# One weight block in four gets its low part from an accumulating DMA instead of a VectorE subtraction

## The chip, the core and the metric

The kernel runs on one core of one Trainium2 chip. The metric is the device time of one execution in microseconds (us). TensorE (PE in the profile) multiplies, VectorE (DVE), ScalarE (ACT) and GpSimd (POOL) work on vectors, SyncE (SP) issues the loads. Each engine takes its own queue of instructions in order and waits on semaphores for what the others make. Every DMA, whoever issues it, runs on the core's 16 DMA engines.

## The reference

Two layers, each of a feed-forward part, a mixer (a state space and an attention beside each other) and a second feed-forward part, over 256 tokens of width 1024, all in float32:

```python
for i in range(DEPTH):                                  # DEPTH = 2
    h = h + 0.5 * swiglu_ffn(rmsnorm(h, norm_ffn1[i]), w_ffn1_in[i], w_ffn1_out[i])
    u = rmsnorm(h, norm_mix[i]) @ w_mix_in[i]           # 1024 -> 6232
    ...
    h = h + jnp.concatenate([y_ssd, y_att], axis=-1) @ w_mix_out[i]
    h = h + 0.5 * swiglu_ffn(rmsnorm(h, norm_ffn2[i]), w_ffn2_in[i], w_ffn2_out[i])
return rmsnorm(h, final_norm)
```

The feed-forward width is 2816, so nearly all the work is the product of 256 tokens with some 208 MB of weights, each of which is read once.

## The kernel before

Each float32 weight is split into two float32r parts whose sum it is, and each main product is three matrix products: x_hi by w_hi, x_hi by w_lo, x_lo by w_hi (lines 181 to 183; 887 to 889 where the weight is the stationary operand).

The weights come as 203 blocks, numbered from 0 in the order of their use, nearly all of 128 partitions by 2048 columns (1 MB). `Stream` handles them. `load` (line 113) issues a block's load from SP into one of three `raw` buffers. `ahead` splits a block: ScalarE casts `raw` to `whi` (line 126), then VectorE makes `wlo` as `raw` minus `whi` (line 127). `whi` and `wlo` have three buffers each. `done` is called when the last product that reads a block has been written down, and it splits the block three further on, into the buffers that come free. So the cast of block b waits until TensorE has finished with block b-3, and the load of block b+3 waits until both readers of `raw` of block b are through.

The order in which TensorE uses the blocks sets how long it takes from a buffer's release to the need for its next content:

- A pair. In the input product of a feed-forward part and in most of the mixer's projection, two blocks (first half and second half of the 1024 rows) belong to the same 512 columns. TensorE reads first half, second half for tokens 0 to 127, then first half, second half for tokens 128 to 255. The first half is released after three quarters of the pair, the second after four. With three buffers, the release after three quarters goes to the second half of the next pair, and that is needed a quarter into that pair: two quarters later. The release after four quarters goes to the first half of the pair after the next, four quarters ahead of its use.
- An output block (256 rows by 1024 columns) is read once through, and is released when TensorE is through with it. The next content of its buffers is needed two blocks later; the last two of a product are read alternately, so that the second of them is needed sooner.

One part of the mixer's projection uses single blocks of 256 columns. The state space's dt chain runs on GpSimd (lines 597 to 610) and ends in a product at line 613. Beside the order of the buffers, a planner orders each engine's instructions by priority and expected times, apart from those that are pinned.

The functions the change touches, and what calls them:

Of the kernel before, what the change touches and what calls it, by code (L numbers as in the profile page):

```python
# [8 lines left out]
F32 = mybir.dt.float32  # L9
FR = mybir.dt.float32r  # L10
I32 = mybir.dt.int32
AF = mybir.ActivationFunctionType
ALU = mybir.AluOpType
AX = mybir.AxisListType

P = 128
D = 1024
# [20 lines left out]
def _pieces12(value, n):  # L38
    """value as n float32 parts of 12 significant bits each (the last one as it comes)."""
    import numpy as np  # L40

    parts, rest = [], float(value)
    for i in range(n):
        p = np.float32(rest)
        if i < n - 1:
            p = (p.view(np.uint32) & np.uint32(0xFFFFF000)).view(np.float32)
        parts.append(float(p))
        rest -= float(p)
    return parts
# [3 lines left out]
def hybrid_kernel(  # L53
# [6 lines left out]
    nc = tc.nc  # L60
# [12 lines left out]

# [1 line left out]
    def bank(pool):  # L75
# [4 lines left out]
    def pin(ins):  # L80
        """Where it matters, an engine takes its instructions in the order given here."""
        return tc.keep_in_program_order(ins) if strict[0] else ins

    def main_bank(wide):
        """The next bank of a main product: one of four, or of two."""
        turns[0] += 1
        return bank(ac if wide and turns[0] % 4 >= 2 else mm)
# [9 lines left out]

    class Stream:
        """The weights, a block at a time in the order of their use: loaded ahead, and split into
        two float32r parts whose sum they are."""  # L100

# [15 lines left out]
        def ahead(self, most=99):  # L117
            while most and self.split < min(self.freed + self.BLOCKS, len(self.plan)):
                self.load()
                n, raw = self.plan[self.split][0], self.raws.pop(0)  # L120
                hi = whl.tile([P, 2048], FR, name="whi", tag="whi")
                lo = whl.tile([P, 2048], FR, name="wlo", tag="wlo")
                parts = 2 if 3 <= self.split < 6 else 1
                for i in range(parts):
                    o = slice(i * n // parts, (i + 1) * n // parts)
                    pin(nc.scalar.copy(hi[:, o], raw[:, o]))  # L126
                    pin(nc.vector.tensor_sub(lo[:, o], raw[:, o], hi[:, o].bitcast(F32)))  # L127
                self.ready.append((hi, lo))
                self.split += 1
                most -= 1  # L130
# [4 lines left out]
        def done(self):  # L135
            """No product will read the oldest block any more."""
            self.freed += 1
            self.ahead()

    class Flow:  # L140
        """Work beside the main products: what was put off at one unit of those comes after the
        next one, and then some steps of the side work."""

# [32 lines left out]
    stream, flow = Stream(), Flow()  # L176

    def three(ps, xhl, t, whi, wlo, first, last):
        """ps += (xh + xl) @ (wh + wl), all but xl @ wl, which float32 does not hold."""
        xh, xl = (v[:, t * P:(t + 1) * P] for v in xhl)  # L180
        nc.tensor.matmul(ps, xh, whi, start=first, stop=False)  # L181
        nc.tensor.matmul(ps, xh, wlo, start=False, stop=False)  # L182
        nc.tensor.matmul(ps, xl, whi, start=False, stop=last)  # L183

# [1 line left out]
    HALVES = ((0, 4), (4, 8))  # L186
# [60 lines left out]
    def project(norm, n, wide=True):  # L247
        """x @ columns, by token: (t, result) as each is there."""
        hl = []
        for t in range(NT):  # L250
            ps = main_bank(wide)[:, :n]
            for i, (k0, k1) in enumerate(HALVES):
                if t == 0:
                    hl.append(stream.take())
                for k in range(k0, k1):
                    hi, lo = (v[:, (k - k0) * n:(k - k0 + 1) * n] for v in hl[i])
                    three(ps, norm.xT[k], t, hi, lo, k == 0, k == KD - 1)
                if t == NT - 1:
                    stream.done()
                if i == 0:  # L260
                    flow.step()
            yield t, ps

    def project_first(norm, n):
        """The same, as the first blocks come: both halves of the tokens side by side."""
        pss = [main_bank(True)[:, :n] for _ in range(NT)]
        for k0, k1 in FIRST:
            hl = stream.take()
            for k in range(k0, k1):
                hi, lo = (v[:, (k - k0) * n:(k - k0 + 1) * n] for v in hl)  # L270
                for t in range(NT):
                    three(pss[t], norm.xT[k], t, hi, lo, k == 0, k == KD - 1)
            stream.done()
        yield from enumerate(pss)

# [1 line left out]
    ones = const.tile([P, P], F32, name="ones")  # L277
    nc.gpsimd.memset(ones, 1.0)
    # the tensor engine is at work before the first operands are there, for its clock's sake
    idle = bank(sd)  # L280
    for _ in range(WARM):
        nc.tensor.matmul(idle[:, 0:P], ones, ones, start=True, stop=True)
    h_res = const.tile([P, NT, D], F32, name="h_res")
# [42 lines left out]

    # cos and sin of the rotary angles, by token: 16 of attention's and 8 of the index's;
    # by use: [cos | cos] and [-sin | sin]
    NF = 24
# [5 lines left out]
    def setup():  # L335
        """What the first products do not need."""
        def later(*a, **k):
# [61 lines left out]
    def rope(eng, v, t, which, nh):  # L399
        """v [P, nh, head dim], in place."""  # L400
        cc, ss, n = ropes[which]
        m1 = row1k()
        m2 = row1k()
        m1 = m1[:, :nh * 2 * n].rearrange("p (h c) -> p h c", h=nh)
        m2 = m2[:, :nh * 2 * n].rearrange("p (h c) -> p h c", h=nh)
        eng.tensor_tensor(m1, v[:, :, 0:2 * n], bc(cc[:, t], [P, nh, 2 * n], 1), ALU.mult)
        eng.tensor_tensor(m2[:, :, 0:n], v[:, :, n:2 * n], bc(ss[:, t, 0:n], [P, nh, n], 1), ALU.mult)
        eng.tensor_tensor(m2[:, :, n:2 * n], v[:, :, 0:n], bc(ss[:, t, n:2 * n], [P, nh, n], 1), ALU.mult)
        eng.tensor_tensor(v[:, :, 0:2 * n], m1, m2, ALU.add)

    def split_scaled(ps, parts, t):
        """Each 128 columns of a bank, times a gain by partition, as two float32r parts."""
        parts = [([v[:, t * P:(t + 1) * P] for v in hl], g, ps[:, i * P:(i + 1) * P])
# [6 lines left out]

# [1 line left out]
    def inv_rms(parts, n, name):  # L422
        """(sum of parts / n + eps) ** -0.5"""
        m = small.tile([P, 1], F32, name=f"ms_{name}", bufs=4)
# [16 lines left out]
    class Norm:  # L441
        """The residual stream, times the gain, as the next product's stationary operand; its
        rms comes into that product's result."""

# [25 lines left out]

# [1 line left out]
    def out_product(yT, n, scale, after, need=None):  # L472
        """h_res += scale * y @ w; yT by 128 rows of w; after(t, c) once a part is done."""
        acc = {}
# [38 lines left out]

# [1 line left out]
    def ffn(first, norm, after):  # L515
# [33 lines left out]

# [1 line left out]
    def mixer(l, norm, after):  # L551
        with ExitStack() as mctx:
# [28 lines left out]

# [1 line left out]
            def steps():  # L583
                """dt = softplus(.) as max(v, 0) + 2 atanh(e / (2 + e)), e = exp(-|v|); the sums of
                dt * a, by token and as rows."""
                if l == 0:
# [41 lines left out]

# [1 line left out]
            def index():  # L630
# [51 lines left out]

# [1 line left out]
            def conv(c, ps):  # L684
# [25 lines left out]

# [1 line left out]
            def ssd():  # L712
# [56 lines left out]
            def finish_y(g, half, pss):  # L769
                """D x, the gate, the norm and the transpose, each some time after the other."""  # L770
                sq = [None] * NT
# [31 lines left out]

# [1 line left out]
            def attention():  # L805
# [70 lines left out]

# [1 line left out]
            flow.until(lambda: not flow.side)  # L878
# [50 lines left out]

# [1 line left out]
    norm = Norm(0, 0)  # L931
# [74 lines left out]
```

## Time and profile before

| | before |
|---|---|
| time, median of 3 runs (lowest to highest) | 1229.9 us (1229.71 to 1231.31) |
| span of the profiled execution | 1227.5 us |
| TensorE matmuls busy | 1207.6 us (98%) |
| VectorE busy | 733.1 us (60%), 452.0 us of it in line 127 |
| ScalarE busy | 623.4 us (51%), 377.5 us of it in line 126 |
| GpSimd busy | 104.7 us (9%) |
| mean load on the DMA engines | 51.9% for SP's queue, 208.52 MB |

Busy times are sums over the whole span. A table like this tells which engine has no room left; it does not tell how long each block's parts are ready before TensorE wants them. That is read block by block in the timeline, below.

### The profile page before, as it was taken

How to read it: one execution, taken by the hardware profiler on the slowest of the kernel's cores; microseconds unless marked ns; L12 is line 12 of the kernel's file. 1: busy time of each engine (PE TensorE's matmuls, PEld its weight loads, DVE VectorE, ACT ScalarE, POOL GpSimd, SP SyncE). 2: the span in 40 equal slices, each digit the busy share in tenths (PEclk: the TensorE clock that was granted, in tenths of full speed). 3: DMA queues.
4: the chain of work that ended last, by engine and by line, in shares of the span. 5: the costliest groups of instructions: out<-in, count | busy, mean ns of one | idle time of the engine just before them, and what ended most of it. 6: DMA issues, size and time to landing. Idle time of an engine off the chain costs nothing.

```text
span 1227.5 us, 15384 instructions
## 1 busy us (share of the span) xinstructions
PE 1207.6 (98%) x6031; PEld 1010.6 (82%) x6031; DVE 733.1 (60%) x970; ACT 623.4 (51%) x856; POOL 104.7 (9%) x209
## 2 busy tenths in 40 slices
PE   8999999999899999999999999999989999999997
PEld 6788889988788888888888888898878888888886
DVE  5655545788478565554465554477766866555543
ACT  5544435556566454444354444365647755444432
POOL 0200000204230000000000000020152200000000
PEclk9999999999999999999999999999999999999999
DMA  8565555564333555655646645565444244556450
GB/s 260 192 206 181 188 175 168 193 202 142 105 136 106 169 184 165 200 198 179 202 152 195 197 168 202 158 212 173 156 154 137 86 172 157 176 182 206 175 202 35
DMA packets 147821, 210.02 MB, mean 171 GB/s; under 512 B 7909, under 2 KB 115109, under 8 KB 147749
## 3 DMA queue, kind: packets, MB, share of 16 engines
q1 hardware_dynamic: 147604, 208.52, 51.9%
q8 instruction: 47, 0.77, 0.3%
q10 hardware_dynamic: 144, 0.52, 0.1%
q14 instruction: 26, 0.20, 0.0%
HBM read 207.98 MB, written 1.05 MB: 170 GB/s over the span
## 4 chain that ended last, share of the span: by engine, by line
PE 90%; DVE 4%; POOL 2%; ACT 1%; issue 1%; DMA 1%; SPq 0%; POOLq 0%; ACTq 0%; DVEq 0%
PE mm L181 14%; PE mm L183 14%; PE mm L182 14%; PE ac L181 12%; PE ac L183 12%; PE ac L182 12%; PE tp L522 2%; DVE wlo L127 1%; PE ac L760 1%; PE sd L821 1%; PE ac L887 1%; PE tp L464 1%; PE mm L889 1%; PE mm L888 1%; PE mm L887 1%
## 5 line engine op out<-in xcount | busy, mean ns | idle before, releaser
L127 DVE TENSOR_TENSOR wlo<-raw,whi 128x2048 fp32r<-128x2048 f32 (+3 forms) x206 | 452.0, 2199 | 326.0 <-ACT whi L126 325.1
L126 ACT CAST whi<-raw 128x2048 fp32r<-128x2048 f32 (+3 forms) x206 | 377.5, 1837 | 303.8 <-PE ac L183 190.5
L181 PE MATMUL mm<-whi,tT 128*128 128x512 f32 (+1 forms) x672 | 269.2, 401 | 0.0
L183 PE MATMUL mm<-whi,tT 128*128 128x512 f32 (+1 forms) x672 | 262.4, 391 | 0.2 <-DVE tT L418 0.2
L182 PE MATMUL mm<-wlo,tT 128*128 128x512 f32 (+1 forms) x672 | 261.2, 389 | 0.0
L181 PE MATMUL ac<-whi,tT 128*128 128x512 f32 (+1 forms) x480 | 189.8, 396 | 1.0 <-ACT tT L416 0.5
L182 PE MATMUL ac<-wlo,tT 128*128 128x512 f32 (+1 forms) x480 | 185.2, 386 | 0.7 <-DVE wlo L127 0.7
L183 PE MATMUL ac<-whi,tT 128*128 128x512 f32 (+1 forms) x480 | 185.3, 386 | 0.0
L183 PEld LDWEIGHTS mm<-whi,tT 128*128 128x128 f32 x672 | 126.8, 189 | 26.3 <-DVE tT L418 0.5
L181 PEld LDWEIGHTS mm<-whi,tT 128*128 128x128 f32 x672 | 127.2, 189 | 25.6 <-issue 1.3
L182 PEld LDWEIGHTS mm<-wlo,tT 128*128 128x128 f32 x672 | 127.4, 190 | 23.0 <-DVE wlo L127 0.2
L182 PEld LDWEIGHTS ac<-wlo,tT 128*128 128x128 f32 x480 | 90.4, 188 | 17.7 <-DVE wlo L127 1.8
L183 PEld LDWEIGHTS ac<-whi,tT 128*128 128x128 f32 x480 | 90.2, 188 | 17.9
L181 PEld LDWEIGHTS ac<-whi,tT 128*128 128x128 f32 x480 | 90.2, 188 | 17.7 <-ACT whi L126 0.9
L432 POOL TENSOR_TENSOR r_x<-ms_x,mhalf 128x1 f32<-128x1 f32 x14 | 9.7, 694 | 873.0 <-DVE ms_x L430 865.4
L181 PE MATMUL ac<-whi,hT_hi 128*128 128x512 f32 x176 | 69.3, 394 | 0.0
L181 PE MATMUL mm<-whi,hT_hi 128*128 128x512 f32 x176 | 69.0, 392 | 0.0
L183 PE MATMUL ac<-whi,hT_lo 128*128 128x512 f32 x176 | 68.6, 390 | 0.0
L183 PE MATMUL mm<-whi,hT_lo 128*128 128x512 f32 x176 | 68.6, 390 | 0.0
L182 PE MATMUL ac<-wlo,hT_hi 128*128 128x512 f32 x176 | 68.5, 389 | 0.0
L182 PE MATMUL mm<-wlo,hT_hi 128*128 128x512 f32 x176 | 68.5, 389 | 0.0
L544 ACT ACTIVATE s1k<-ac,r_x 128x256 f32<-128x256 f32 x44 | 20.6, 471 | 67.6 <-PE ac L183 64.7
(220 smaller groups left out, 1447.3 us busy)
## 6 DMA issues: line engine op xcount, KB each, us to landing
raw<-in_w_ffn_in_dram SPq DMA_DIRECT2D x172, 512.0 KB, 5.0
raw<-in_w_ffn_out_dram SPq DMA_DIRECT2D x44, 1024.0 KB, 4.9
raw<-in_w_mix_in_dram SPq DMA_DIRECT2D x44, 1024.0 KB, 5.3
raw<-in_w_mix_out_dram SPq DMA_DIRECT2D x16, 1024.0 KB, 4.9
raw<-in_w_mix_in_dram SPq DMA_DIRECT2D x4, 600.0 KB, 3.9
raw<-in_w_mix_in_dram SPq DMA_DIRECT2D x4, 568.0 KB, 3.9
raw<-in_w_ffn_in_dram SPq DMA_DIRECT2D x8, 256.0 KB, 3.7
h_res<-in_x_dram SPq DMA_DIRECT2D x4, 256.0 KB, 3.9
```

The lines of the kernel that those rows point to most:

```text
L126: pin(nc.scalar.copy(hi[:, o], raw[:, o]))
L127: pin(nc.vector.tensor_sub(lo[:, o], raw[:, o], hi[:, o].bitcast(F32)))
L181: nc.tensor.matmul(ps, xh, whi, start=first, stop=False)
L182: nc.tensor.matmul(ps, xh, wlo, start=False, stop=False)
L183: nc.tensor.matmul(ps, xl, whi, start=False, stop=last)
L464: nc.tensor.transpose(ps[:, i * P:(i + 1) * P], src[:, i * P:(i + 1) * P], ident)
L522: nc.tensor.transpose(ps[:, f * L + t * P:f * L + (t + 1) * P], hs[:, t, f * P:(f + 1) * P], ident)
L544: nc.scalar.activation(sg, ps[:, 0:256], AF.Silu, scale=norm.r[t])
L760: nc.tensor.matmul(o, m0[:, h % 4, t * P:(t + 1) * P], half[:, 0, h * 64:(h + 1) * 64], start=True, stop=(t == 0))
L821: nc.tensor.matmul(ps[:, j * nk:(j + 1) * nk], qT[:, hg + h0 + j, t * P:(t + 1) * P], kT[:, hg + h0 + j, 0:nk], start=True, stop=True)
L887: nc.tensor.matmul(ps, hi[:, o:o + P], xh, start=(k == 0), stop=False)
L888: nc.tensor.matmul(ps, hi[:, o:o + P], xl, start=False, stop=False)
```

## The change

For blocks with a number above 16 that leaves 1 when divided by 4, and that have 2048 columns, the split is made in three steps: ScalarE casts `raw` to `whi` as before, ScalarE writes the negative of `whi` into `wlo`, and GpSimd issues a DMA that adds `raw` to `wlo` in place. The subtraction on VectorE is left out for these blocks. The changes of comments in the diff do nothing.

```diff
                 parts = 2 if 3 <= self.split < 6 else 1
+                if self.split > 16 and self.split % 4 == 1 and n == 2048:
+
+                    nc.scalar.copy(hi, raw)
+                    nc.scalar.activation(lo, hi.bitcast(F32), AF.Copy, scale=-1.0)
+                    nc.gpsimd.dma_start(lo, raw, accum_op=ALU.add)
+                    parts = 0
                 for i in range(parts):
                     o = slice(i * n // parts, (i + 1) * n // parts)
                     pin(nc.scalar.copy(hi[:, o], raw[:, o]))
                     pin(nc.vector.tensor_sub(lo[:, o], raw[:, o], hi[:, o].bitcast(F32)))
```

That picks 45 of the 203 blocks (37 and 137 are narrower than 2048): second halves of pairs in the second feed-forward parts (73, 77, 81, 85, 89 and 173 to 189), first halves in the first feed-forward parts (17, 21 and 105 to 121), in the projection the first halves 41, 45, 49 and the second halves 53, 57, 61 (141 to 161 in the second layer), and the output blocks 25, 29, 33, 65, 69, 93, 97, 101 (each again 100 later).

## Rows read from the trace of the kernel before

**Rows 1.** The page: busy us (share of the span) xinstructions, by engine.
```profile
PE 1207.6 (98%) x6031; PEld 1010.6 (82%) x6031; DVE 733.1 (60%) x970; ACT 623.4 (51%) x856; POOL 104.7 (9%) x209
```

**Rows 2.** Waits, all engines: engine line waited for: us in total, times, longest us.
```profile
DVE wlo L127 <- ACT whi L126: 325.1, 161, 5.7
...
PE sd L613 <- POOL adt L610: 7.0, 2, 3.5
...
PE ac L182 <- DVE wlo L127: 0.7, 1, 0.7
```

**Rows 3.** Waits of SP's own queue of DMAs.
```profile
SPq L113 <- DVE wlo L127: 774.6, 114, 15.2
```

**Rows 4.** Timeline, block 73: start, us, engine, line, operation [idle before <-releaser].
```profile
439.09 1.91 ACT L126 CAST whi<-raw 128x2048 fp32r<-128x2048 f32 x1 [0.37 <-PE mm L183]
...
441.03 2.29 DVE L127 TENSOR_TENSOR wlo<-raw,whi 128x2048 fp32r<-128x2048 f32 x1 [1.15 <-ACT whi L126]
...
444.87 0.39 PE L182 MATMUL mm<-wlo,tT 128*128 128x512 f32 x1
```

**Rows 5.** Timeline, block 189, the last of the ten like block 73.
```profile
1136.31 2.29 DVE L127 TENSOR_TENSOR wlo<-raw,whi 128x2048 fp32r<-128x2048 f32 x1 [3.24 <-ACT whi L126]
...
1140.11 0.39 PE L182 MATMUL mm<-wlo,tT 128*128 128x512 f32 x1
```

**Rows 6.** Timeline, block 69, last output block of the mixer.
```profile
414.57 2.29 DVE L127 TENSOR_TENSOR wlo<-raw,whi 128x2048 fp32r<-128x2048 f32 x1 [3.19 <-ACT whi L126]
...
419.41 0.39 PE L182 MATMUL mm<-wlo,tT 128*128 128x512 f32 x1
```

**Rows 7.** Timeline, block 57, a second half in the projection.
```profile
317.75 2.29 DVE L127 TENSOR_TENSOR wlo<-raw,whi 128x2048 fp32r<-128x2048 f32 x1 [5.74 <-ACT whi L126]
...
323.28 0.40 PE L182 MATMUL mm<-wlo,tT 128*128 128x512 f32 x1
```

**Rows 8.** Timeline, block 41, a first half in the projection.
```profile
214.73 2.29 DVE L127 TENSOR_TENSOR wlo<-raw,whi 128x2048 fp32r<-128x2048 f32 x1 [2.42 <-ACT whi L126]
...
220.66 0.40 PE L182 MATMUL mm<-wlo,tT 128*128 128x512 f32 x1
```

**Rows 9.** Timeline, block 93, second output block of a feed-forward part.
```profile
555.03 2.29 DVE L127 TENSOR_TENSOR wlo<-raw,whi 128x2048 fp32r<-128x2048 f32 x1 [3.24 <-ACT whi L126]
...
561.56 0.39 PE L182 MATMUL mm<-wlo,hT_hi 128*128 128x512 f32 x1
```

**Rows 10.** Timeline, block 61, the last second half in the projection.
```profile
354.77 2.29 DVE L127 TENSOR_TENSOR wlo<-raw,whi 128x2048 fp32r<-128x2048 f32 x1 [0.17 <-ACT whi L126]
...
362.34 0.40 PE L182 MATMUL mm<-wlo,tT 128*128 128x512 f32 x1
```

**Rows 11.** Timeline, block 97, an output block in the steady run.
```profile
574.62 2.29 DVE L127 TENSOR_TENSOR wlo<-raw,whi 128x2048 fp32r<-128x2048 f32 x1 [3.15 <-ACT whi L126]
...
583.58 0.39 PE L182 MATMUL mm<-wlo,hT_hi 128*128 128x512 f32 x1
```

**Rows 12.** Timeline, block 109, a first half in a feed-forward part.
```profile
642.42 2.29 DVE L127 TENSOR_TENSOR wlo<-raw,whi 128x2048 fp32r<-128x2048 f32 x1 [0.43 <-ACT whi L126]
...
652.14 0.39 PE L182 MATMUL ac<-wlo,tT 128*128 128x512 f32 x1
```

**Rows 13.** The page's DMA issues: output<-input, engine, count, KB each, median us to landing.
```profile
raw<-in_w_ffn_out_dram SPq DMA_DIRECT2D x44, 1024.0 KB, 4.9
...
out_dram<-h_res SPq DMA_DIRECT2D x4, 128.0 KB, 1.9
```

**Rows 14.** Windows: stretch, length, busy by engine, granted clock, DMA share, GB/s.
```profile
304.00:308.00 4.00, 2.48 (x16) 1.91 (x14) 0.61 (x1) 1.65 (x3) 3.18 (x10) 1.00 0.99 353
312.00:316.00 4.00, 4.00 (x12) 3.17 (x12) 0.01 (x1) 0.43 (x2) 0.92 (x3) 0.62 0.00 0
```

**Rows 15.** Timeline of GpSimd: one of its slowest small operations, and one of its many short ones.
```profile
300.41 2.15 POOL L601 TENSOR_SCALAR sp_p<-sp_z 128x32 f32<-128x32 f32 x1
...
304.85 0.26 POOL L604 TENSOR_TENSOR sp_p<-sp_p,sp_z 128x32 f32<-128x32 f32 x1
```

## The prediction

> **What bounds the kernel now.** I read the page's first section, then the waits, then the timeline around single blocks. TensorE's matmuls are busy 98% of the span, VectorE 60% and ScalarE 51% [rows 1]; the span is 1227.5 us, the median of the runs 1229.9, so some 2.4 us lie around the profiled span. The list of waits says how the split stands to TensorE: VectorE idles 325.1 us for the cast, yet TensorE's wait for a low part is 0.7 us in the whole run [rows 2]. So TensorE is the bound, and the subtraction that the change takes away is not on the path: its cost now is nothing. What can change the time is only whether the new low part still comes before TensorE wants it. That is not a sum of busy times but a slack for each block: the start of the first matmul that reads `wlo` (line 182), minus the end of the subtraction.
>
> Block 73 shows the chain. The cast starts at 439.09, released by TensorE's last read of the buffer, and takes 1.91; the subtraction starts 0.03 us after it and ends at 441.03 + 2.29 = 443.32; the first low product starts at 444.87 [rows 4]. The slack is 1.55 us. For the last of the ten blocks of this kind it is 1140.11 - 1138.60 = 1.51 [rows 5]. Worked out in the same way:
> - ten second halves in the second feed-forward parts: 1.5 [rows 4, 5]
> - 69 and 169: 2.55 [rows 6]; 57 and 157: 3.25 [rows 7]; 41 and 141: 3.65 [rows 8]; 93 and 193: 4.25 [rows 9]; 61 and 161: 5.3 [rows 10], and 53 and 153 I take like these
> - eight output blocks in the steady run: 6.65 [rows 11]
> - eleven blocks like the first half 109: 7.4 [rows 12].
> These are 41 of the 45. Blocks 45, 65 and their two twins have more than any of these and are left out.
>
> **The change part by part.** Removed: 45 subtractions of 2.29 us on VectorE, 103 us of an engine that waits anyway. Nothing is gained by that directly. One indirect gain: the dt chain of the mixer, which passes over VectorE, keeps TensorE waiting 3.5 us at line 613 in each layer [rows 2], and block 53's subtraction lies ahead of it. I count no more for it than that this gap swallows a stall of block 53 just before it, up to 3.5 us in each layer.
>
> Added on ScalarE: 45 negations, which have the cast's shape and I price at the cast's 1.91 us [rows 4], plus 0.03 for the hand-over. Their 86 us fit into an engine that is 51% busy [rows 1]; behind the negation stands the next block's cast, which belongs to a first half with 7.4 us of slack, so nobody waits. On the path of its own block the negation counts in full: 1.94.
>
> Added on GpSimd: the issue of a DMA. No row shows one. The lower bound is a short GpSimd operation, 0.26 us, the upper a slow one, 2.15 [rows 15]. I take 1.0, between them, since writing out a transfer for 128 partitions should be more than the shortest operation. Queued behind it on GpSimd is hardly anything in the feed-forward parts (the engine is 9% busy [rows 1]); in the mixer it can hold up the rotary and dt work by as much as it waits for ScalarE, which I price at nothing, as that work has other waits.
>
> Added on the DMA engines: a 1 MB transfer that must read `raw` and `wlo` and write `wlo`. No row shows an accumulating transfer. A plain 1 MB load lands in 4.9 us [rows 13]. With the engines 99% busy they move 353 GB/s [rows 14], so 1 MB (1.05 million bytes) takes 3.0 us, and 1.9 of the 4.9 is fixed. From below: as cheap as a plain load, 4.9. From above: three passes one after another, 1.9 + 9.0 = 10.9. I take two passes, because there are two reads and the write can go on beside them: 1.9 + 6.0 = 7.9. The nearest row, the plain load, is the lower end, and a second operand cannot come for nothing. A gain below the removed 2.3 us is excluded but for a landing in under 1.9 us, which is what a transfer of an eighth of the size takes [rows 13].
>
> Does this transfer collide with loads? Hardly: SP's next load waits for `raw` of the same block (SP's waits for line 127 are 774.6 us in all [rows 3]), so it comes behind the accumulation. That load then lands some 18 us after the block's release (0.4 + 1.9 + 1.9 + 1.0 + 7.9 + 4.9). In the pairs its cast is released five quarters of a pair after block 73's, 14 us by the 5.8 from cast to first use that two quarters take [rows 4], and the stall below comes on top, so it is no second stall.
>
> Together, the low part comes later than before by X = 1.94 + 1.0 + 7.9 - 2.32 = 8.5 us.
>
> The Trainium skill, "Collectives: The Full Stack", section "The bandwidth ceiling: the fold count and why AG ≠ RS ≠ AR", says that an add in the DMA path needs two read descriptors for each chunk on the same ring and so runs at about half the rate of a copy, while the adding itself costs no cycles. No row here shows it. With the fit for a plain transfer in "DMA: Bandwidth & Descriptors", section "Anatomy of one DMA", 2.0 us plus bytes over 436 GB/s, two reads would be an estimate of 6.8 us, X would be 7.4 in place of 8.5, and the time, by the sum below, about 1355.
>
> **The sum.** Each block stalls TensorE by X minus its slack, and as TensorE is the bound each stall moves everything behind it, so stalls add: 10 x 7.0 = 70; 2 x 5.95 = 11.9 (69); 2 x 5.25 = 10.5 (57); 2 x 4.85 = 9.7 (41); 2 x 4.25 = 8.5 (93); 2 x 3.2 = 6.4 (61); 53 is swallowed; 8 x 1.85 = 14.8 (output); 11 x 1.1 = 12.1. That is 144 us.
>
> A second term is TensorE's clock. After the 3.5 us idle stretch at line 613 the granted clock over 312 to 316 us is 0.62 of full, between the levels of 1.2 and 2.4 GHz, with TensorE fully busy [rows 2, 14]: (1 - 0.62) x 4 = 1.5 us lost. I charge 1.5 us to each stall about as long as that one or longer: 10 + 2 + 2 + 2 + 2 = 18 stalls (61 is just below, and 53 takes a gap's place), 27 us. Shorter stalls I charge nothing.
>
> Forecast: 1229.9 + 144 + 27 = 1401 us.
>
> **The rivals.**
> A. The accumulation costs what a plain load costs and the issue next to nothing: X = 1.94 + 0.3 + 4.9 - 2.32 = 4.8. Then 10 x 3.3 + 2 x (2.25 + 1.55 + 1.15 + 0.55) = 44 us and stalls too short for the clock: 1274. If it is between this and the forecast, X = 6, the same working gives 45 + 2 x (3.45 + 2.75 + 2.35 + 1.75 + 0.7) = 67, with 15 for the clock at the ten: 1312. For it: `wlo` and `raw` are both on the chip, without the way to the main memory. Against: two operands.
> B. The passes do not overlap, or the adder is slower than the copy: X = 1.94 + 1.0 + 10.9 - 2.32 = 11.5. Then 100 + 2 x (8.95 + 8.25 + 7.85 + 7.25 + 6.2 + 2.7) + 8 x 4.85 + 11 x 4.1 = 266, and with the clock at 39 stalls 58: 1554. For it: nothing shows that the write is hidden. A fourth pass adds 3 us to each of 41 stalls, 123 us more.
> C. It is not slower. The place is the ten second halves with the least slack; the price of the new low part is then at most the slack, X under 1.5, which wants a landing under 1.9 us with a short issue. What then shows is VectorE's relief ahead of line 613: at most the subtraction of block 53, 2.3 us in each layer, 1225. Against it: a transfer eight times smaller already takes 1.9 us [rows 13].
> D. The change does not do what it says, for instance because the condition picks no block: 1230. By the lengths of the plan it picks 45.
>
> **How the numbers follow.** The forecast of two overlapped reads has 45% (its own range, X from 7 to 10, about 1345 to 1470), A with what lies toward it 22%, B 27%, C 4%, D 2%. The range takes most of A's upper part and of B: 1290 to 1590. About 0.2% is what a measurement of this kernel can tell from no change. Faster by more than that is C, 3%; within it is D and the edge of C, 3%; slower 94%.
>
> **What would show it.** In the profile of the changed kernel, TensorE should wait for a DMA into `wlo` ahead of line 182, some 7 us at each of the ten second halves in the second feed-forward parts and hardly at all at the first halves of the first ones. The time to landing of the accumulating transfer decides between A, the forecast and B: 4.9, 7.9, 10.9. GpSimd's issue should be near 1 us. VectorE should have 45 fewer instructions in line 127 and ScalarE 45 more; the clock should be at its lower level for some us behind each long stall. I am wrong if the waits stand elsewhere (at line 181 for `whi`, or on ScalarE or SP for `raw`), if loads run beside the accumulation and both grow, or if GpSimd's queue, not the transfer, is what the low part waits for.

## The result

The changed kernel takes 1352.2 us (median; 1349.6 to 1353.8) against 1230.6 us before, a ratio of 1.0984 with a 95% interval of 1.0970 to 1.0999. It is slower by some 122 us; the forecast was 171 us slower, 1401, in a range of 1290 to 1590. Lines from 127 on have moved: the negation is line 127, the accumulating DMA 128, the old cast and subtraction 132 and 133, the three products 187 to 189.

The page of the changed kernel: busy time by engine, the queue of the accumulating DMA, groups (line engine op, out<-in, count | busy, mean ns | idle before, releaser), and DMA issues with the median from issue to landing.

```profile
span 1351.0 us, 15557 instructions
PE 1252.8 (93%) x6031; PEld 1031.8 (76%) x6031; DVE 631.0 (47%) x925; ACT 704.2 (52%) x901; POOL 130.9 (10%) x254
...
q0 software_dynamic: 6480, 47.19, 18.2%
...
L128 POOL DMA_DIRECT2D wlo<-raw x45 | 39.5, 877 | 864.7 <-ACT wlo L127 809.4
...
L127 ACT ACTIVATE wlo<-whi 128x2048 fp32r<-128x2048 f32 x45 | 86.1, 1914 | 0.8
...
raw<-in_w_ffn_in_dram SPq DMA_DIRECT2D x172, 512.0 KB, 5.6
wlo<-raw POOLq DMA_DIRECT2D x45, 1024.0 KB, 7.8
raw<-in_w_ffn_out_dram SPq DMA_DIRECT2D x44, 1024.0 KB, 6.2
```

VectorE lost 45 instructions and 102 us of work beside [rows 1], ScalarE gained the negations at 1.91 us each, GpSimd 45 issues of 0.88 us. The accumulating transfer lands 7.8 us (median) after GpSimd begins to issue it. Against [rows 13] the output product's loads now land in 6.2 us in place of 4.9: they were delayed too.

The span grew by 123.5 us. TensorE's busy time grew by 45.2 us (1207.6 to 1252.8) though it runs the same 6031 matmuls: that is the lower clock, seen below. The other 78 us are new idle time. What TensorE waits for in the changed kernel (us in total, times, longest):

```profile
PE mm L188 <- DMA wlo<-raw: 64.0, 24, 4.5
PE tp L644 <- POOL s L415: 7.2, 2, 3.6
PE sd L619 <- POOL adt L616: 5.4, 2, 2.7
PE ac L188 <- DMA wlo<-raw: 4.5, 5, 1.8
PE ac L893 <- ACT whi L132: 2.8, 2, 1.4
```

The waits for the new low part are 68.5 us in all, where the kernel before waited 0.7 us for it [rows 2]. The second and the fifth row are new as well and are not waits for a low part; the run without blocks 41 and 141 comes back to them.

Block 73, to be held against [rows 4], in the timeline of the changed kernel:

```profile
472.88 1.91 ACT L126 CAST whi<-raw 128x2048 fp32r<-128x2048 f32 x1 [0.34 <-PE mm L189]
474.82 1.92 ACT L127 ACTIVATE wlo<-whi 128x2048 fp32r<-128x2048 f32 x1
...
477.03 0.88 POOL L128 DMA_DIRECT2D wlo<-raw  x1 [6.09 <-ACT wlo L127]
...
478.40 0.39 PE L187 MATMUL mm<-whi,tT 128*128 128x512 f32 x1
478.63 0.39 PE L187 MATMUL ac<-whi,tT 128*128 128x512 f32 x1
...
481.50 0.48 PE L187 MATMUL ac<-whi,tT 128*128 128x512 f32 x1
485.10 0.79 PE L188 MATMUL mm<-wlo,tT 128*128 128x512 f32 x1 [3.12 <-DMA wlo<-raw]
485.69 0.63 PE L189 MATMUL mm<-whi,tT 128*128 128x512 f32 x1
```

The chain is the one forecast: cast, negation, 0.3 us to the issue, 8.1 us from the issue to the first product that reads the result. Two things were not in the forecast. From 478.63 on TensorE runs products of the other bank (`ac`): the 12 products of the first half for tokens 128 to 255, a transpose and, at 481.50, one product of the second half; in the order of the text these come after the ones that wait. The planner has put them ahead. And the products behind the wait take 0.63 us where they took 0.39: the windows say why (columns as in [rows 14]).

```profile
480.00:484.00 4.00, 1.98 (x10) 1.29 (x8) 1.77 (x3) 2.38 (x2) 0.00 (x0) 1.00 1.04 164
484.00:488.00 4.00, 2.90 (x7) 2.33 (x8) 2.37 (x2) 0.00 (x0) 0.00 (x0) 0.54 0.96 323
488.00:492.00 4.00, 4.00 (x13) 3.13 (x12) 0.49 (x1) 0.47 (x1) 0.00 (x0) 0.61 1.10 349
```

The granted clock is 0.54 and 0.61 in the stretches behind the idle time, near the lower of its two levels (0.50).

### The profile page after: what moved, and what is told of

Read it like the earlier page. It is cut to its first block, busy times and chain, and to the rows that moved or that the text cites. A ratio compares the mean times of both kernels' runs of the same rounds, so it can differ in the third digit from the quotient of the medians.

```text
span 1351.0 us, 15557 instructions
## 1 busy us (share of the span) xinstructions
PE 1252.8 (93%) x6031; PEld 1031.8 (76%) x6031; DVE 631.0 (47%) x925; ACT 704.2 (52%) x901; POOL 130.9 (10%) x254
## 3 DMA queue, kind: packets, MB, share of 16 engines
q0 software_dynamic: 6480, 47.19, 18.2%
## 4 chain that ended last, share of the span: by engine, by line
PE 61%; DMA 23%; ACT 7%; issue 6%; POOL 2%; DVE 1%; SPq 0%; POOLq 0%; ACTq 0%; DVEq 0%
DMA wlo<-raw 21%; PE mm L188 10%; PE mm L189 10%; PE mm L187 9%; PE ac L188 8%; PE ac L189 8%; PE ac L187 7%; ACT wlo L127 2%; ACT whi L126 2%; DMA raw<-in_w_ffn_in_dram 1%; ACT whi L132 1%; PE ac L766 1%; POOL sp_p L609 1%; PE tp L528 1%; PE tp L470 1%
## 5 line engine op out<-in xcount | busy, mean ns | idle before, releaser
L133 DVE TENSOR_TENSOR wlo<-raw,whi 128x2048 fp32r<-128x2048 f32 (+2 forms) x161 | 348.4, 2168 | 449.0 <-ACT whi L132 448.6
L132 ACT CAST whi<-raw 128x2048 fp32r<-128x2048 f32 (+2 forms) x161 | 290.7, 1810 | 225.7 <-PE ac L189 150.4
L188 PE MATMUL mm<-wlo,tT 128*128 128x512 f32 (+1 forms) x672 | 276.7, 412 | 59.6 <-DMA wlo<-raw 59.6
L187 PE MATMUL mm<-whi,tT 128*128 128x512 f32 (+1 forms) x672 | 279.2, 416 | 0.0
L189 PE MATMUL mm<-whi,tT 128*128 128x512 f32 (+1 forms) x672 | 273.8, 407 | 0.3 <-DVE tT L424 0.3
L188 PEld LDWEIGHTS mm<-wlo,tT 128*128 128x128 f32 x672 | 134.3, 200 | 91.7 <-DMA wlo<-raw 67.1
L189 PEld LDWEIGHTS mm<-whi,tT 128*128 128x128 f32 x672 | 134.3, 200 | 27.7 <-DVE tT L424 0.7
L187 PEld LDWEIGHTS mm<-whi,tT 128*128 128x128 f32 x672 | 132.9, 198 | 27.8 <-issue 1.3
L126 ACT CAST whi<-raw 128x2048 fp32r<-128x2048 f32 x45 | 86.3, 1917 | 76.4 <-PE mm L189 40.6
L128 POOL DMA_DIRECT2D wlo<-raw x45 | 39.5, 877 | 864.7 <-ACT wlo L127 809.4
L127 ACT ACTIVATE wlo<-whi 128x2048 fp32r<-128x2048 f32 x45 | 86.1, 1914 | 0.8
```

What stands on the lines that cost most here:

```text
L126: nc.scalar.copy(hi, raw)
L127: nc.scalar.activation(lo, hi.bitcast(F32), AF.Copy, scale=-1.0)
L128: nc.gpsimd.dma_start(lo, raw, accum_op=ALU.add)
```

## The experiments

All runs start from the changed kernel unless said otherwise. The theory: each block stalls TensorE by X, the lateness of its low part, less its slack and less what the planner can put in between, and a long stall also costs clock. The rivals: an equal price for each transfer (load on the DMA engines, GpSimd's queue), or ScalarE's second pass.

**Which blocks hold the loss.** The condition was narrowed to the ten second halves of the second feed-forward parts, and to the other 35.

```diff
-                if self.split > 16 and self.split % 4 == 1 and n == 2048:
+                if self.split in (73, 77, 81, 85, 89, 173, 177, 181, 185, 189):
```

> Only the ten second halves of pairs in the second feed-forward parts (73 to 89, 173 to 189) take the accumulating path; the other 35 blocks keep the subtraction. My theory: the loss is where the low part comes later than its slack, so these ten hold what the trace of the changed kernel shows at them, ten idle stretches of about 3.1 us and some 21 us of half-clock work behind them, 52 us of the 122: about 1282 us. Rival, that each accumulating transfer costs the same by loading the DMA engines and GpSimd's queue: 10 of 45 parts of 122 us, 27 us: about 1257 us.

Measured: 1283.5 us, 53 us over before, with 1282 forecast. TensorE's waits:

```profile
PE mm L188 <- DMA wlo<-raw: 30.8, 10, 3.3
```

Ten waits of 3.1 us; the remaining 22 us are the clock (TensorE's busy time rises by 25 us over before).

> The other way round: the 35 blocks without those ten. My theory: 122 - 52 = 70 us more than before, about 1300 us, most of it in the mixers, hardly any at first halves and output blocks. Rival of an equal price for each transfer: 35 of 45 parts, 95 us, about 1325 us. If this and the run with the ten alone do not add up to the whole 122 us, the two groups act on each other, which neither theory says.

Measured: 1306.5 us, 76 us over before. 53 and 76 make 129, a little over the whole 122, so the groups hardly act on each other. Ten transfers cost 5.3 us each, thirty-five 2.2 us each, so the rival of an equal price is out.

**What the planner's order is worth.** The products of the ten pairs were held in the order of the text.

```diff
+        hold = tc.keep_in_program_order if held[0] else (lambda ins: ins)
-        nc.tensor.matmul(ps, xh, whi, start=first, stop=False)
+        hold(nc.tensor.matmul(ps, xh, whi, start=first, stop=False))
```

> All 45 blocks as in the changed kernel, but in those ten pairs TensorE's products are held in the order in which they are written. In the changed kernel the planner puts the 12 products of the first half for the second tokens ahead of the waiting ones; held, about 11 of them (2.5 us) come behind. My theory, that this swap covered part of the late low part: each of the ten idle stretches grows from 3.1 to about 5.6 us, 25 us in all, about 1377 us with the clock as it was. Rival, that the transfer was simply faster for these blocks than I had reckoned and the swap does nothing: 1352 us.

Measured: 1377.4 us, 25 us more than the changed kernel. The held kernel's waits of TensorE have a new row beside those for the DMA:

```profile
PE mm L189 <- DMA wlo<-raw: 60.7, 24, 4.5
PE tp L531 <- DVE hs L554: 25.2, 10, 2.5
```

A transpose that now stands ahead of the waiting product waits 2.5 us at each of the ten, so the idle time there is about 5.3 us in two parts, where it was 3.1 in one. The 12 products did cover about that much.

**The price of adding.** The DMA copies and does not add.

```diff
-                    nc.gpsimd.dma_start(lo, raw, accum_op=ALU.add)
+                    nc.gpsimd.dma_start(lo, raw)
```

> The same order of all instructions, but GpSimd's DMA copies raw to wlo without adding (the low part is then the raw block: part of the computation is changed). My theory, two reads at the rate of the engines: the landing falls from 7.8 by the 3.0 us of one read to about 4.8, X from 7.8 to 4.8; the stalls at the ten all but vanish and with them the clock's loss: about 1255 us. Rival, that the time is GpSimd's issue and the fixed part of a transfer inside the chip, or an adder that costs nothing: landing stays near 7 and the time near 1340 us.

Measured: 1248.5 us. Its page:

```profile
q0 software_dynamic: 6480, 47.19, 10.0%
...
wlo<-raw POOLq DMA_DIRECT2D x45, 1024.0 KB, 4.3
```

The copy lands in 4.3 us in the median, the accumulation in 7.8; the fastest of each take 4.1 and 6.9. GpSimd's issue of the copy takes 0.53 us in the median, of the accumulation 0.87. The difference of 3.5 us (2.8 between the fastest) less these 0.34 is what adding costs, 2.5 to 3.2 us, near the 3.0 that a megabyte takes with the engines full [rows 14]. The queue's share of the engines falls from 18.2% of 1351 us to 10.0% of 1245, 246 to 125 us, a half. Time and queue share together fit a second read. No wait of TensorE for the DMA is left. Most of the 18 us over before are the mixer's: the waits at lines 644 and 893 are still there, 7.2 and 2.8 us, and are taken up next.

**GpSimd's queue.** Blocks 41 and 141 keep the subtraction.

> The changed kernel without blocks 41 and 141, which keep the subtraction: 43 blocks. My theory: in GpSimd's queue the DMA of block 41 waits for the negation ahead of the rotary work of the index, so that TensorE waits 3.6 us for that work (line 644) in each layer and a low clock follows; without the two blocks that goes, with the 1.4 to 2 us of their own stalls: about 18 us less, 1333 us. Rival, that this wait comes from the later timing of the mixer as a whole and not from GpSimd's queue: only the two stalls go, about 1348 us.

Measured: 1336.2 us, 16 us less, and the waits at lines 644 (7.2 us) and 893 (2.8 us) are gone from TensorE's list; the waits for the DMA are only 2.2 us less. The timelines show how the wait at line 644 came about. In the kernel before, GpSimd's rotary work for the index starts here:

```profile
211.76 0.62 POOL L406 TENSOR_TENSOR s1k<-s,cc_idx 128x144 f32<-128x144 f32 x1 [6.35 <-ACT s L904]
```

In the changed kernel it stands behind the DMA of block 41, which waits for ScalarE's negation first:

```profile
222.37 0.89 POOL L128 DMA_DIRECT2D wlo<-raw  x1 [13.18 <-ACT wlo L127]
225.89 0.10 POOL L692 MEMSET xr<- 128x3 f32 x1 [2.62 <-DVE s1k L702]
225.95 0.48 POOL L412 TENSOR_TENSOR s1k<-s,cc_idx 128x144 f32<-128x144 f32 x1
...
230.60 0.69 PE L644 MATMUL tp<-ident,s 128*128 128x128 f32 x2 [3.64 <-POOL s L415]
```

The DMA is not the whole of the delay. Behind it stands an instruction of the convolution (line 692) that waits another 2.62 us for VectorE; in the kernel before, it came behind the first token block's rotary work. The run below that makes the negation first keeps both DMAs in GpSimd's queue, has no other wait between them and the rotary work, and shows no wait at line 644. So a waiting DMA and the planner's order behind it cost this together.

**The negation alone.** VectorE adds `raw` to the negated part.

```diff
-                    nc.gpsimd.dma_start(lo, raw, accum_op=ALU.add)
+                    nc.vector.tensor_add(lo, raw, lo.bitcast(F32))
```

> The negation on ScalarE stays, but VectorE adds raw to it instead of the DMA, in the same 45 blocks. It prices the negation alone. My theory: X is 1.94 us plus nothing, over the slack of 1.5 us only at the ten second halves, by some 0.4 us, and no clock loss: 1230 to 1236 us. Rival, that the second pass of ScalarE over each block, and what it holds up in ScalarE's queue, is a large part of the 122 us: 1250 us or more.

Measured: 1236.2 us, a ratio of 1.0049 (1.0032 to 1.0066). ScalarE's second pass costs 5 us; the other 116 come with the DMA, its lateness and its place in GpSimd's queue. Here TensorE waits neither at line 644 nor at line 893.

**Less lateness.** ScalarE makes the negative straight from `raw` and the cast comes last.

```diff
-                    nc.scalar.copy(hi, raw)
-                    nc.scalar.activation(lo, hi.bitcast(F32), AF.Copy, scale=-1.0)
-                    nc.gpsimd.dma_start(lo, raw, accum_op=ALU.add)
+                    nc.scalar.activation(lo, raw, AF.Copy, scale=-1.0)
+                    nc.gpsimd.dma_start(lo, raw, accum_op=ALU.add)
+                    nc.scalar.copy(hi, raw)
```

> ScalarE writes the negative of the cast straight from raw into wlo, the accumulating DMA is issued after that, and the cast to whi comes last. X falls by the 1.9 us of one ScalarE pass, from 7.8 to 5.9. If TensorE's order stayed, every stall would be 1.9 us shorter and most of the clock's loss gone, about 1290 us. But in this kernel the planner puts only 4 products ahead of the waiting ones instead of 12, 1.6 to 1.8 us less cover, so at the ten second halves I expect about 3 us of idle time as before, and the gain only at the other blocks: about 1325 us. Rival, that the planner's order has no weight: 1290 us.

Measured: 1319.1 us, near the 1325 of the theory with the planner. But it is near by compensation. The idle stretches at the ten were about 2 us and not 3, and the waits at lines 644 and 893 went too, 10 us that the forecast did not name; the waits for the DMA fell by 10 us at the ten and rose by 2 at the other blocks, where an earlier transfer can run into the loads, as the run with the 23 blocks shows below.

**Two halves.** Negation and DMA by 1024 columns.

```diff
+                    for o in (slice(0, 1024), slice(1024, 2048)):
+                        nc.scalar.activation(lo[:, o], hi[:, o].bitcast(F32), AF.Copy, scale=-1.0)
+                        nc.gpsimd.dma_start(lo[:, o], raw[:, o], accum_op=ALU.add)
```

> As the changed kernel, but negation and accumulating DMA in two halves of 1024 columns each, so that TensorE can begin with the first half. My theory, a landing of a fixed part plus two reads: 1.9 + 3.0 us and GpSimd's issue, about 4.8 to 5.3 us for half a block in place of 7.8, and the second half some 3 us behind the first. The planner here puts only 2 products ahead of the waiting ones instead of 12, so at the ten second halves some 2 to 2.5 us of idle time stay of 3.1, mostly too short for the clock: about 1320 us. Rival, that the landing is mostly a fixed price of the accumulating path: over 6.5 us for each half, one behind the other, and the time above 1352 us.

Measured: 1303.6 us. Half a block lands in 4.5 us at the least and 6.2 in the median, so the rival of a fixed price is out. The forecast was 16 us too cautious.

**The clock.** In the ten pairs, 22 products of constant tiles stand ahead of the waiting one.

```diff
+                    if i == 1 and stream.freed + 1 in (73, 77, 81, 85, 89, 173, 177, 181, 185, 189):
+                        fill = bank(sd)
+                        for _ in range(22):
+                            tc.keep_in_program_order(nc.tensor.matmul(fill[:, 0:P], ones, ones, start=True, stop=True))
```

> All 45 blocks as in the changed kernel, but in the ten pairs 22 products of two constant tiles (0.21 us each, 4.7 us, their result is not used) stand ahead of the waiting ones, and TensorE's order there is again the written one. So the idle stretch of 5.6 us of the kernel with the held order (1377 us) is filled with work that gives nothing but keeps TensorE busy. My theory, that the clock falls because of the idle time and costs there about half of ten stretches of 6.8 us: the clock stays at its upper level at the ten and the time falls by 22 to 32 us, to about 1350 us. Rival, that the lower clock has another cause, or costs nothing since the wait is for the DMA: 1377 us or more.

Measured: 1369.6 us, 8 us under the held order and not 22 to 32. The windows around block 73 in this kernel and, below, in the held one:

```profile
484.00:488.00 4.00, 2.64 (x16) 2.07 (x15) 0.00 (x0) 0.00 (x0) 0.00 (x0) 1.00 0.93 242
488.00:492.00 4.00, 4.00 (x20) 3.26 (x19) 1.17 (x2) 0.95 (x2) 0.00 (x0) 1.00 0.99 316
```

```profile
478.00:482.00 4.00, 1.22 (x4) 0.49 (x4) 1.09 (x3) 0.58 (x1) 0.00 (x0) 0.61 0.98 166
482.00:486.00 4.00, 3.76 (x10) 3.01 (x11) 0.00 (x0) 0.00 (x0) 0.00 (x0) 0.54 1.09 363
```

The mechanism holds: with the idle stretch filled, the clock stays at its upper level. The size was wrong, because I had taken 5.6 us as the wait in both. Here nothing useful is done meanwhile, and filling, the single product behind it and the rest of the wait make 6.4 us at each of the ten, against 5.3 in the held kernel: 11 us more idle or filled time, so the clock gave back about 19 us, an estimate from these two sums, 1.9 for each stall.

**Where the low part has room.** The quicker order, only in 23 blocks with a slack before of 6.6 us or more.

> The accumulating path, negation first, only in 23 blocks whose slack before was 6.6 us or more (first halves in the first feed-forward parts, output blocks in the steady run, 45, 49, 65 and twins). X is 5.9 us, so by my theory nothing waits: 1230 to 1235 us. Rival of an equal price for each transfer (89 us for the 45 with the negation first): 23 of 45 parts, 45 us, about 1275 us.

Measured: 1252.3 us, 22 over before: the forecast was wrong. TensorE still waits for the DMA, 14 us in eleven places of 0.7 to 1.9, and the clock falls after one of them. The transfer's times to landing, for the first halves of the second layer's first feed-forward part and then for the last two output blocks:

```profile
DMA to landing us min/median/max: 8.5/11.3/11.7
...
DMA to landing us min/median/max: 6.9/7.0/7.0
```

And the windows around one of those first halves, issued while the weight loads run:

```profile
655.00:658.00 3.00, 3.00 (x16) 2.45 (x15) 1.17 (x2) 0.95 (x2) 0.00 (x0) 1.00 0.99 287
658.00:661.00 3.00, 3.00 (x15) 2.49 (x14) 0.00 (x0) 1.91 (x1) 0.00 (x0) 1.00 1.00 209
```

The DMA engines are full (0.99 and 1.00 in the column after the clock). Issued 1.9 us earlier, the accumulation meets the loads of the next blocks, and lands in 8.5 to 11.7 us; the same five landed in 7.2 to 9.1 us in the changed kernel, and one alone takes 7. What the earlier issue gives, the collision takes. So X is not one number for all blocks.

**Using it where VectorE is in the way.** TensorE's one long wait in the kernel before stands at the end of the dt chain [rows 2], with VectorE's subtractions in the queue ahead of it. The quicker order, only in blocks 51, 52, 54, 56 and their twins:

> The accumulating path, negation first, in eight blocks alone: 51, 52, 54, 56 and their twins in the second layer, whose subtractions stand in VectorE's queue ahead of the dt chain that TensorE waits for (3.5 us in each layer of the kernel before, and a low clock behind it). Their slack there is 10.0, 6.6, 6.2 and 14.3 us, over the X of 5.9 us. If the subtractions hold up that chain, up to 2.3 us for each of them goes from the chain and the wait goes away: 1220 to 1226 us. Rival, that GpSimd's queue (the DMAs stand in it among the rotary work, waiting for ScalarE) or the planner's other order takes that back: 1230 us or more.

Measured: 1229.6 us, a ratio of 1.000 (0.999 to 1.001). The wait for the chain is gone from the list, but 5.9 us of waits for the DMA have come, 2.4 us the longest, with a landing of 9.0 us in the median. One wait was traded for another. Then, in the same quicker order, only 51, 56 and twins:

```diff
-                if self.split > 16 and self.split % 4 == 1 and n == 2048:
+                if self.split in (51, 56, 151, 156):
```

> Of the eight blocks of the run in the mixers only 51, 56 and their twins, which have the most slack (10.0 and 14.3 us), so that no low part comes late even where a transfer lands in 11 us beside the weight loads. If the subtraction of block 56 beside the dt chain on GpSimd (one of its 0.3 us operations takes 2.1 us there) and that of block 51 on VectorE hold up the chain, the wait of 3.5 us at its end shrinks to under 2 us in each layer and the low clock behind it goes: 1222 to 1226 us. Rival, that what the eight blocks gave came from 52 and 54 alone, or that the chain only moves: 1229 to 1231 us, no change.

Measured: 1225.5 us, a ratio of 0.9961 (0.9947 to 0.9975): 0.4% faster than the kernel before. TensorE's waits:

```profile
PE sd L619 <- POOL adt L616: 3.8, 2, 2.1
PE sd L288 <- POOL ones L284: 1.1, 1, 1.1
```

No wait for the DMA, and the wait for the chain is 3.8 us in both layers together where it was 7.0. The timelines say where that comes from. In the kernel before, VectorE subtracts blocks 55 and 56 one after the other beside the chain, and two of GpSimd's short operations take over 2 us, that of [rows 15] and the next:

```profile
300.10 4.51 DVE L127 TENSOR_TENSOR wlo<-raw,whi 128x2048 fp32r<-128x2048 f32 x2
...
302.64 2.12 POOL L603 TENSOR_SCALAR sp_p<-sp_p 128x32 f32<-128x32 f32 x1
```

Without the subtraction of block 56, one of the two is short again:

```profile
301.51 2.30 DVE L133 TENSOR_TENSOR wlo<-raw,whi 128x2048 fp32r<-128x2048 f32 x1
...
301.82 2.15 POOL L607 TENSOR_SCALAR sp_p<-sp_z 128x32 f32<-128x32 f32 x1
304.05 0.29 POOL L609 TENSOR_SCALAR sp_p<-sp_p 128x32 f32<-128x32 f32 x1
```

From its first operation on GpSimd to its last, the chain takes 10.1 us where it took 11.9, in either layer. So it is the subtraction of block 56 running beside the chain, not one waiting ahead of it in VectorE's queue, that shortens it. The low clock behind the wait went in the second layer alone, where the wait is 1.7 us: 0.60 over 916 to 920 us before, 1.00 from 912 to 920 us here. It stayed in the first (2.1 us of wait; 0.72 over 312 to 316 us). Block 51 alone was not tried.

## Why the prediction came out as it did

- **The bound and the mechanism** were right: VectorE's relief is worth nothing where TensorE waits for nothing, and the low part comes too late. Narrowing the blocks shows where the low part is late, and adding on VectorE shows that the DMA makes it so.
- **The lateness.** X was 8.5 us; it is 1.94 + 0.3 + 7.8 - 2.32 = 7.7. Issue and transfer were priced at 8.9 and take 8.1 with the hand-over. That two reads set the transfer's time fits the copy. The Trainium skill, "Collectives: The Full Stack", section "The bandwidth ceiling: the fold count and why AG ≠ RS ≠ AR", says it of a reduce-scatter between cores; the 2.5 to 3.2 us that adding costs here agree with it within one core. The estimate of 6.8 us for two reads, from that and from the fit in the Trainium skill, "DMA: Bandwidth & Descriptors", section "Anatomy of one DMA", is near the 7.0 us that one transfer takes alone, issue included. That 6.8 and 1.0 for the issue make just the median of 7.8 is luck, since the median is of transfers that mostly ran beside loads.
- **The ten second halves** are the term that failed most: 7.0 us each was forecast, 3.1 us of idle time came. 7.7 less the slack of 1.5 is 6.2; the 12 products that the planner moved ahead, a transpose and one product more take 3.1 of that. The step that failed is that I took TensorE's order to be the one of the text, though it is said above that a planner orders each engine. In the trace of the kernel before, TensorE does take these pairs in the order of the text; the planner moved the products only in the changed kernel. The held order shows it. For 69 and 169, forecast 5.95 and measured 2.1, the cause is probably the same, but that was only read from the order.
- **The clock.** 27 us was forecast, from 18 stalls at 1.5. TensorE's busy time rose by 45 us. Shorter stalls (2 to 3 us) were also followed by the lower level, and each costs more than 1.5: 2.2 by the run with the ten alone. The stalls were priced too high and the clock too low.
- **GpSimd's queue** was priced at nothing, "as that work has other waits". Blocks 41 and 141 cost 16 us: 7.2 of waits at line 644 and 2.8 at line 893, 2.2 of waits for the DMA, and some 2 of clock. The step that failed is that I named who stands behind the waiting DMA and did not follow who waits for them: the index's transposes on TensorE.
- **Block 53** was to be swallowed by the gap of the dt chain. It was not: TensorE waited 3.6 and 2.1 us there and another 2.7 at the chain's end in each layer. The chain hangs on more than VectorE's queue, and came later too.
- **Loads.** "Hardly" any collision holds only for the output blocks in the steady run (landings of 6.9 to 7.0 us). The ten second halves landed in 7.7 to 8.3, the first halves of the feed-forward parts in up to 9.1 (11.7 when issued earlier), 57 and 61 in 9.5 and 9.4, and 41 and 141 in 10.2 and 10.8. The prediction's own sign for this came: the loads of the output product grew too, from 4.9 to 6.2 us. It had looked at the load that waits for `raw` of the same block alone. A load that waits for the next block's `raw` comes sooner: for block 73, VectorE finishes block 74 at 480.85, and SP issues into the buffer that comes free while the accumulation runs until about 485. It was also the step that broke the forecast for the 23 blocks.

```profile
478.56 2.29 DVE L133 TENSOR_TENSOR wlo<-raw,whi 128x2048 fp32r<-128x2048 f32 x1 [4.87 <-ACT whi L132]
...
480.88 1.77 SPq L113 DMA_DIRECT2D raw<-in_w_ffn_in_dram  x2
```

- **The sum.** 144 us of stalls and 27 of clock became 78 and 45, and 10 of the 78 are the waits at lines 644 and 893, which the sum did not have. The time of about 1355 us that the two pages gave is near the measured one, but by compensation: its sum also counted without the planner. With either of the two errors alone the time would still have been in the range, which was wide. The waits for the low part, row by row:

| blocks | forecast, us | measured, us |
|---|---|---|
| ten second halves | 70 | 31.1 |
| 69, 169 | 11.9 | 4.3 |
| 57, 157 | 10.5 | 7.4 |
| 41, 141 | 9.7 | 3.3 |
| 93, 193 | 8.5 | 3.3 |
| 61, 161 | 6.4 | 6.9 |
| 53, 153 | 0 | 5.6 |
| nineteen with most slack in the sum (steady output blocks, first halves) | 26.9 | 6.5 |

Of the nineteen, the output blocks 29, 33, 97, 101 and their twins did not wait at all: alone on the engines they land in 7.0 us, so that X is 6.9 there, close to the slack of 6.65. Why 93 and 193 wait so little was not followed.

## What to carry to other kernels

Before work moves off a busy engine, read the slack of each piece, not the engine's share: a step that ends 1.5 us before its use can't become one that takes 8. An accumulating DMA of 1 MB cost here 2.5 to 3.2 us more than a copy, and a place in GpSimd's queue, where it holds up what stands behind it while it waits. It paid here only for four blocks with room, two of which had been subtracted beside a chain that the bound waits for. And a planner's queue order is part of the kernel and can change with the edit: count with it, and look at it in the new trace before adding stalls up.

## What was unexpected of the hardware

- The accumulating transfer of 1 MB within the chip lands in 7.0 us with the engines to itself, about 8 beside some traffic and up to 11.7 beside weight loads; a copy of the same size lands in 4.3 in the median.
- Issuing the accumulation holds GpSimd for 0.87 us in the median, the copy for 0.53.
- GpSimd's short operations of the dt chain take 0.2 to 0.6 us. In the kernel before and in the last run, those that started while VectorE subtracted a block (2.3 us) took 2.1 to 2.2 us and ended 0.2 us behind the subtraction.
- An idle stretch of about 3 us of TensorE was followed by 0.54 and 0.61 of the full clock in the two stretches of 4 us around and behind its end, and each such stall cost some 2.2 us of clock. With two idle parts of 2.5 and 2.8 us it was some 1.9; 4.7 us of useless products in place of most of that kept the clock at 1.00.
